# The split input of a feed-forward up-projection in lines of 128 bytes: high halves of 16 tokens beside their low halves

## The chip, the cores and the metric

One Trainium2 chip, one core. The time of a kernel is the device time of one execution in microseconds (us); the number that counts is the median over runs. A profiled execution gives a trace, and the page and the answers quoted here are read from it. Engines are named as the profile names them: PE (matrix engine, matmuls), PEld (its weight loads), DVE (vector), ACT (scalar), POOL (GpSimd), SP (the queue that issues most transfers).

## What is computed

One decoder layer on 256 tokens of 2048 features: two token mixers merged by gates, a cross-attention into 256 memory tokens, and a channel mixer. Each of the three adds a normed result to the residual stream. The change touches the channel mixer:

```python
def conv_glu_ffn(h, w_up, conv_w, conv_b, w_down):
    u = h @ w_up                                   # 256x2048 @ 2048x16384: the up-projection
    uc = conv_b + sum(conv_w[j] * shift_right(u, CONV_WIDTH - 1 - j) for j in range(CONV_WIDTH))
    gate, up = split_cols(uc, (D_FF, D_FF))        # D_FF = 8192
    return (jax.nn.gelu(gate, approximate=True) * up) @ w_down

h = rms_norm(x, ffn_pre_norm[l])
x = x + rms_norm(conv_glu_ffn(h, ...), ffn_post_norm[l])
```

Everything is float32.

## The kernel before

**Products in three parts.** Every large matrix product is split: an operand is stored as a high half, rounded to the type that the profile prints as fp32r (four bytes an element, as float32), and a low half, what the rounding left. A product is then three matmuls that add into one PSUM tile: high weights with high input, high weights with low input, low weights with high input. ACT makes the high half of the weights (`wh`, line 391), DVE the low half (`wl`, line 421).

**The stream of weights.** All weights pass PE once, in the order in which the program needs them, as pieces of 128 partitions by 1024 numbers (512 KB): `Feed` loads a piece (`raw`), and `hi` and `lo` split it into `wh` and `wl`. The pieces are counted from 0 through the whole program (`i` in `Feed.staged`). The order of work is written out by the program: `run()` goes through the blocks and issues matmuls, and `Spread` slips the other engines' work in between by a fixed budget. There is no scheduler behind it.

**The up-projection.** It is 32 blocks of kind "fm", each with eight pieces of 2 x 512 weights. Features lie on partitions: in each matmul 128 x 128 weights are the stationary operand, and 256 tokens of one group of 128 features are the moving operand. So there are 32 x 8 x 2 x 4 = 2048 weight tiles of each half, and 3 x 2048 = 6144 matmuls of 256 columns, each with a weight load of its own. The moving operands are the tiles `fh` and `fl` (high and low half of the normed residual stream): 16 groups of features x 256 tokens each, so that one matmul reads 256 numbers that follow each other, 1024 bytes in each partition. The same holds for the earlier "fm" blocks with `hh`, `hl` (mixers) and `mh`, `ml` (memory tokens).

**The down-projection** is of kind "tm": there the input (`as`) is stationary, and 512 columns of weights move.

**Where operands start.** The tiles of the moving inputs start at a multiple of 128 bytes. `Feed.staged` puts a piece of weights 16 numbers (64 bytes) into its buffer, so that weights of "fm" blocks start 64 bytes past a multiple of 128. For 19 pieces the table `KICK` moves them: by 24 numbers (96 bytes) instead of 16, or with eight numbers more between the two groups of features in the piece, or both.

```python
o = 0 if c >= 512 and self.kind[i] == "tm" else 16
if kick is not None:
    o, e = ((24, e + 24), (o, e + 8), (24, e))[kick]
```

None of the 19 pieces belongs to the up-projection (pieces 264 to 519).

**What makes fh and fl.** When the cross-attention's statistic is there, `Residual.run` scales and adds the residual stream group by group: ACT writes the high half (`act.activation`), DVE the low half (`scalar_tensor_tensor`). The very first group is made in two halves of the tokens by DVE alone, since PE waits for it. `Residual.tile(k)` hands group k to the matmuls. After the up-projection the buffers of `fh` and `fl` (tag `hT`, two buffers) are used again for the last norm's gain and for half of its result (`z3`).

Of the kernel before, what the change touches and what calls it, by code (L numbers as in the profile page):

```python
# [9 lines left out]
F32 = mybir.dt.float32  # L10
F32R = mybir.dt.float32r
AF = mybir.ActivationFunctionType
# [3 lines left out]
P = 128  # L16
D = 2048
S = 256
# [127 lines left out]
def _layer(ctx, tc, nc, d, dbg):  # L146
# [15 lines left out]
    def big(name, shape=None, dt=F32):  # L162
        return mp.tile(shape or [P, KD, S], dt, tag="big", bufs=2, name=name)

    def hT(name):
        return mp.tile([P, KD, S], F32R, tag="hT", bufs=2, name=name)

    def C(name, tag, shape=None, dt=F32):
        return mp.tile(shape or [P, S], dt, tag=tag, bufs=1, name=name)
# [8 lines left out]
        return pp.tile(shape or [P, 512], F32, tag="aux", bufs=4, name=name)  # L178

    def mm(out, lhsT, rhs, start=True, stop=True):  # L180
        pe.matmul(out, lhsT, rhs, start=start, stop=stop, skip_group_check=True)  # L181

    def keep_warm(n):
# [13 lines left out]
    def pcol(n, i=0, w=1):  # L197
        return par[:, PC[n] + i:PC[n] + i + w]
# [395 lines left out]
        return [d[name][blk, c] for c in range(d[name].shape[1])]  # L594


    hh, hl = hT("hh"), hT("hl")
    xs0 = lambda k: (hh[:, k], hl[:, k])
    st0 = Stat("st0")

# [897 lines left out]
    def part(v, k2):  # L1498
        return v[k2 // 4][:, (k2 % 4) * 2:(k2 % 4) * 2 + 2]

    class Residual:
# [8 lines left out]
        def run(self):  # L1510
            st, key, hi, lo, gname = self.a
            z, xr = M[key], M["xr"]
            for _ in range(10):
                if st.done:
                    break
                yield
            while not st.done:
                side._piece(side.bulk[0])
            rb = st.rb
            if not self.early:  # L1520
                keep_warm(5)

            def parts(i, js=(0, 1)):
                for j in js:
                    k = i * 2 + j
                    act.activation(hi[:, k], part(xr, i)[:, j], AF.Identity, scale=pcol(gname, k))
                for j in js:
                    k = i * 2 + j
                    dve.scalar_tensor_tensor(lo[:, k], part(xr, i)[:, j], pcol(gname, k), hi[:, k],
                                             op0=ALU.mult, op1=ALU.subtract)  # L1530
                self.ready = i + 1

            def scale(i):
                dve.tensor_mul(part(z, i), part(z, i), bc(rb, 2))

            def add(i):
                dve.tensor_add(part(xr, i), part(xr, i), part(z, i))

            if self.early:
                yield  # L1540
            a, x = part(z, 0), part(xr, 0)
            for j in range(2):
                if j == 0 and not self.early:
                    for t in TH:
                        dve.tensor_mul(a[:, 0, t], a[:, 0, t], rb[:, t])
                    for t in TH:
                        dve.scalar_tensor_tensor(hi[:, 0, t], a[:, 0, t], pcol(gname, 0), M["xg"][:, 0, t],
                                                 op0=ALU.mult, op1=ALU.add)
                else:
                    dve.tensor_mul(a[:, j], a[:, j], rb)  # L1550
                dve.tensor_add(x[:, j], x[:, j], a[:, j])
                if j == 0 and not self.early:
                    dve.scalar_tensor_tensor(lo[:, 0], x[:, 0], pcol(gname, 0), hi[:, 0], op0=ALU.mult,
                                             op1=ALU.subtract)
            if self.early:
                scale(1)
                parts(0)
            else:
                parts(0, (1,))
                scale(1)  # L1560
            yield
            for i in range(1, 8):
                if i == 1:
                    add(1)
                if i < 7:
                    scale(i + 1)
                    add(i + 1)
                parts(i)
                if i == 1 and not self.early:
                    side.more()  # L1570
                if self.early:
                    self.st2.add(part(xr, i - 1))
                    if i == 7:
                        self.st2.add(part(xr, 7))
                        self.stats = side.add(self.st2.early_column(), chain=1, free=True)
                elif i == 6:
                    self.stats = side.add(self.squares(), chain=1)
                yield
# [48 lines left out]
    stm = Stat("stm", "ysb0")  # L1627

    def mem_prep():
        M["mh"], M["ml"] = hT("mh"), hT("ml")  # L1630
        ts = []
        for c in range(10):
            if c % 2 == 0 and c < 8:
                ts.append(C("mem", f"bg{c // 2 % 2}", [P, 4, S]))
                sp.dma_start(ts[c // 2], d["mem"][:, c * 2:c * 2 + 4])
            if c >= 2:
                t = ts[c // 2 - 1][:, c % 2 * 2:c % 2 * 2 + 2]
                for j in range(2):
                    k = c * 2 - 4 + j
                    split_gain(M["mh"][:, k], M["ml"][:, k], t[:, j], pcol("mg", k))  # L1640
                stm.add(t)
            yield
        yield from stm.finish()
# [164 lines left out]
    def start_ffn():  # L1808
        M["cv"] = C("cv", "ysb0", [P, 4, P])
        act.dma_start(M["cv"], d["conv"])  # L1810
        side.need(xo3["task"])
        M["res"] = Residual(st3, "z2", stf, hT("fh"), hT("fl"), "fg", False)

    M["ac"] = []

# [106 lines left out]
                yield  # L1922

    def load_gain():
        M["gain"] = mp.tile([P, D], F32, tag="hT", bufs=2, name="gain")
        sp.dma_start(M["gain"], d["fpg"].partition_broadcast(P))

    E4 = [slice(0, S), slice(S, 2 * S)]
# [1 line left out]
    def fd_evac(n):  # L1930

        def gen(ps):
            if n:
                z = mp.tile([P, 2, 1024], F32, tag="hT", bufs=2, name="z3")
            else:
                z = U("z3", [P, 2, 1024])
            M["z3", n] = z

            if n == 0:
                M["ssq"], M["rco"] = small("ssq", [P, 2, 4], bufs=1), small("rco", [P, 2], bufs=1)  # L1940
            ssq, rco = M["ssq"], M["rco"]

            def squares(g):
                jk = T2("jk", [P, 512])
                act.activation(jk, ps[g], AF.Square, accum_out=ssq[:, g // 2, n * 2 + g % 2:n * 2 + g % 2 + 1])

            def gain(g):
                c = slice(g % 2 * 512, g % 2 * 512 + 512)
                dve.tensor_mul(z[:, g // 2, c], ps[g], M["gain"][:, n * 1024 + c.start:n * 1024 + c.stop])

            def before_last(t):
                ss = M["sso"] = small("sso", [P, 1], bufs=2)
                dve.tensor_reduce(ss, ssq[:, t, 0:3], axis=AX.X, op=ALU.add)
                dve.tensor_scalar(ss, ss, 1.0 / D, EPS, op0=ALU.mult, op1=ALU.add)

            def finish(t):
                r = rco[:, t:t + 1]
                act.activation(r, ssq[:, t, 3:4], AF.Ln, scale=1.0 / D, bias=M["sso"])
                act.activation(r, r, AF.Exp, scale=-0.5)

            def result(t, c):
                f = slice(c % 2 * 512, c % 2 * 512 + 512)
                x, z_ = M["xt"][c // 2][:, t, f], M["z3", c // 2][:, t, f]
                if t and c == 0:
                    diag = C("diag", "ysb0", [P, P])
                    act.activation(diag, ident, AF.Copy, scale=rco[:, t:t + 1])
                    for q, v in zip(M["sum"], E4):
                        mm(q, diag, z_[:, v], start=False)
                    for q, v in zip(M["sum"], E4):
                        act.copy(x[:, v], q)  # L1970
                else:
                    dve.scalar_tensor_tensor(x, z_, rco[:, t:t + 1], x, op0=ALU.mult, op1=ALU.add)
                (act if t and c == 0 else sp).dma_start(d["out"][t, :, c * 512:c * 512 + 512], x)

            if n == 0:
                for g in range(4):
                    squares(g)
                    gain(g)
                    yield
                return  # L1980
            squares(0)
            before_last(0)
            gain(0)
            squares(1)
            finish(0)
            gain(1)
            result(0, 0)
            result(0, 1)
            squares(2)
# [12 lines left out]
            yield  # L2002
        return gen
# [97 lines left out]
```

## Time and profile before

| what | value |
|---|---|
| runs, median (lowest to highest) | 1866.33 us (1866.29 to 1867.76), 3 runs |
| profiled execution, first to last instruction | 1863.2 us |
| PE busy | 1853.5 us, 99% of the span |
| DVE, ACT, POOL busy | 1295.5, 1017.0, 32.4 us |
| granted PE clock, mean | 0.999 of full |
| up-projection, first to last matmul start | 806.6 to 1507.2 us |
| bytes read | 347.01 MB, 187 GB/s over the span |

The profiled execution has no time of its own in the list of runs; its span is 3.1 us below their median, and this rest, what lies before the first and behind the last instruction, is added to spans below to compare them with runs. Busy time of PE is no measure of its speed, since one matmul's recorded 276 ns overlaps the next two: what a matmul costs is the distance from one start to the next.

### The profile page before, as it was taken

The numbers are of one execution on the slowest core, as the hardware profiler recorded it, in microseconds if no ns is written. First come the engines' busy times: TensorE is split into PE (matmuls) and PEld (weight loads), VectorE is DVE, ScalarE is ACT, GpSimd is POOL, SyncE is SP. The second block draws the span as 40 slices with busy tenths as digits, with TensorE's granted clock in tenths as the row PEclk, the third lists the DMA queues.
The fourth block names the chain that finished last, engine by engine and source line by source line (L and its number), as shares of the span: only waits on it lengthen the run. The fifth ranks groups of instructions, "written<-read, shape, count | busy, mean of one in ns | idle before, by whom it ended". The sixth has DMA issues, their size and how long they took to land.

```text
span 1863.2 us, 36212 instructions
## 1 busy us (share of the span) xinstructions
PE 1853.5 (99%) x14934; PEld 1767.5 (95%) x14934; DVE 1295.5 (70%) x1832; ACT 1017.0 (55%) x1492; POOL 32.4 (2%) x62
## 2 busy tenths in 40 slices
PE   9999999999999999999999999999999999999998
PEld 9999988999999999999999999999999988888887
DVE  7789777566675857787766667776666775556555
ACT  6876445655454646665554455444445554545544
POOL 0000020000000000000000000000000000000000
PEclk9999999999999999999999999999999999999999
DMA  7556544344555765555666666666666666666664
GB/s 261 186 166 203 180 149 160 136 160 158 172 195 196 277 197 180 165 180 172 202 192 194 196 195 196 185 194 199 195 194 195 197 192 215 194 193 192 194 192 145
DMA packets 98198, 351.47 MB, mean 189 GB/s; under 512 B 11056, under 2 KB 11568, under 8 KB 97648
## 3 DMA queue, kind: packets, MB, share of 16 engines
q1 hardware_dynamic: 97168, 348.01, 58.6%
q8 instruction: 117, 1.92, 0.4%
q10 hardware_dynamic: 864, 1.15, 0.2%
q14 instruction: 49, 0.40, 0.1%
HBM read 347.01 MB, written 2.10 MB: 187 GB/s over the span
## 4 chain that ended last, share of the span: by engine, by line
PE 98%; DVE 1%; DMA 0%; issue 0%; ACT 0%; ACTq 0%; DVEq 0%
PE fm L181 68%; PE tm L181 25%; PE gram L181 0%; DVE wl L421 0%; PE Y L181 0%; DMA w<-in_w_in_dram 0%; PE num L181 0%; PE lv L181 0%; DVE ql L66 0%; PE X L181 0%; PE U L181 0%; PE zg L181 0%; DVE z L66 0%; PE zwa L181 0%; PE xsc L181 0%
## 5 line engine op out<-in xcount | busy, mean ns | idle before, releaser
L421 DVE TENSOR_TENSOR wl<-raw,wh 128x1024 fp32r<-128x1024 f32 (+1 forms) x639 | 774.8, 1218 | 412.7 <-ACT wh L391 406.5
L391 ACT CAST wh<-raw 128x1024 fp32r<-128x1024 f32 (+1 forms) x639 | 663.6, 1043 | 476.0 <-PE fm L181 362.5
L181 PE MATMUL fm<-fh,wh 128*128 128x256 f32 x2048 | 564.2, 277 | 0.6 <-DVE fh L66 0.6
L181 PE MATMUL fm<-fh,wl 128*128 128x256 f32 x2048 | 563.2, 276 | 0.0
L181 PE MATMUL fm<-fl,wh 128*128 128x256 f32 x2048 | 563.2, 276 | 0.0
L181 PEld LDWEIGHTS fm<-fh,wh 128*128 128x128 f32 x2048 | 383.6, 188 | 0.8 <-DVE fh L66 0.8
L181 PEld LDWEIGHTS fm<-fl,wh 128*128 128x128 f32 x2048 | 383.5, 188 | 0.0
L181 PEld LDWEIGHTS fm<-fh,wl 128*128 128x128 f32 x2048 | 383.5, 188 | 0.0
L181 PE MATMUL tm<-wh,as 128*128 128x512 f32 x1024 | 315.1, 389 | 0.0
L181 PE MATMUL fm<-hh,wh 128*128 128x256 f32 x1024 | 284.3, 280 | 1.7 <-ACT wh L402 1.5
L181 PE MATMUL fm<-hl,wh 128*128 128x256 f32 x1024 | 281.7, 277 | 0.0
L181 PE MATMUL fm<-hh,wl 128*128 128x256 f32 x1024 | 281.5, 277 | 0.1
L181 PEld LDWEIGHTS tm<-wh,as 128*128 128x128 f32 x1024 | 192.2, 188 | 39.8
L181 PE MATMUL tm<-wl,as 128*128 128x512 f32 x512 | 199.2, 389 | 0.0
L181 PEld LDWEIGHTS fm<-hh,wh 128*128 128x128 f32 x1024 | 191.9, 188 | 3.4 <-ACT wh L402 1.7
L181 PEld LDWEIGHTS fm<-hl,wh 128*128 128x128 f32 x1024 | 191.9, 188 | 0.1
L181 PEld LDWEIGHTS fm<-hh,wl 128*128 128x128 f32 x1024 | 191.5, 188 | 0.3 <-DVE wl L421 0.3
L181 PEld LDWEIGHTS tm<-wl,as 128*128 128x128 f32 x512 | 96.1, 188 | 19.9
L66 ACT CAST as<-ac 128x256 fp32r<-128x256 f32 x128 | 45.6, 404 | 110.8 <-PE tm L181 110.8
L66 DVE TENSOR_TENSOR as<-ac,as 128x256 fp32r<-128x256 f32 x128 | 48.6, 421 | 61.7 <-ACT as L66 61.7
L181 PE MATMUL fm<-mgh,wh 128*128 128x256 f32 x256 | 70.9, 277 | 0.0
L181 PE MATMUL fm<-mgl,wh 128*128 128x256 f32 x256 | 70.8, 276 | 0.0
(406 smaller groups left out, 2225.0 us busy)
## 6 DMA issues: line engine op xcount, KB each, us to landing
raw<-in_w_fu_dram SPq DMA_DIRECT2D x256, 512.0 KB, 4.1
raw<-in_w_in_dram SPq DMA_DIRECT2D x152, 512.0 KB, 3.6
raw<-in_w_fd_dram SPq DMA_DIRECT2D x128, 512.0 KB, 3.9
raw<-in_w_br_dram SPq DMA_DIRECT2D x32, 512.0 KB, 4.1
raw<-in_w_mo_dram SPq DMA_DIRECT2D x32, 512.0 KB, 4.3
raw<-in_w_xk_dram SPq DMA_DIRECT2D x8, 512.0 KB, 4.2
raw<-in_w_xv_dram SPq DMA_DIRECT2D x8, 512.0 KB, 3.6
raw<-in_w_xq_dram SPq DMA_DIRECT2D x8, 512.0 KB, 4.0
```

The costliest lines, as they stand in the source:

```text
L66: return f(out, *a, **k)
L181: pe.matmul(out, lhsT, rhs, start=start, stop=stop, skip_group_check=True)
L391: nc.scalar.copy(wh, r)
L421: nc.vector.tensor_sub(wl, r, self.st[self.nl][0])
```

## The change

The two tiles of a split input become one tile of twice the size. For the mixers and for the memory tokens (`hpair`) the high half fills its first 16 KB of a partition and the low half its second, so a matmul reads there what it read before (1024 bytes in a row). For the up-projection (`hlines`) the tile is cut into lines of 32 numbers (128 bytes): 16 tokens' high halves in a line's first 64 bytes, the same tokens' low halves in its second. A matmul of the up-projection then reads 16 runs of 64 bytes, 128 bytes apart, in place of one run of 1024 bytes; `mm` gives its PSUM output the same shape of 16 x 16. What ACT and DVE write there has this pattern too, 16 runs of 16 numbers (8 runs in the first group's halves). The last norm's gain and `z3` become parts of one tile `hend` in the same place.

```diff
-    def hT(name):
-        return mp.tile([P, KD, S], F32R, tag="hT", bufs=2, name=name)
+    def hT(name, dt=F32R):
+        return mp.tile([P, 2 * KD * S], dt, tag="hT", bufs=1, name=name)
+
+    def hpair(name):
+        v = hT(name).rearrange("p (i k s) -> p i k s", i=2, k=KD)
+        return v[:, 0], v[:, 1]
+
+    def hlines(name):
+        v = hT(name).rearrange("p (k l i w) -> p i k l w", k=KD, i=2, w=W16)
+        return v[:, 0], v[:, 1]
+
+    W16 = 16
+
+    def lines(v):
+        return v.rearrange("p (l w) -> p l w", w=W16)
...
     def mm(out, lhsT, rhs, start=True, stop=True):
+        if len(rhs.shape) == 3 and len(out.shape) == 2 and rhs.shape[2] == W16:
+            out = lines(out)
         pe.matmul(out, lhsT, rhs, start=start, stop=stop, skip_group_check=True)
...
-    hh, hl = hT("hh"), hT("hl")
+    hh, hl = hpair("hp")
...
+            as_hi = (lambda v: v) if self.early else lines
...
-                    act.activation(hi[:, k], part(xr, i)[:, j], AF.Identity, scale=pcol(gname, k))
+                    act.activation(hi[:, k], as_hi(part(xr, i)[:, j]), AF.Identity, scale=pcol(gname, k))
...
-                    dve.scalar_tensor_tensor(lo[:, k], part(xr, i)[:, j], pcol(gname, k), hi[:, k],
+                    dve.scalar_tensor_tensor(lo[:, k], as_hi(part(xr, i)[:, j]), pcol(gname, k), hi[:, k],
                                              op0=ALU.mult, op1=ALU.subtract)
...
-                        dve.scalar_tensor_tensor(hi[:, 0, t], a[:, 0, t], pcol(gname, 0), M["xg"][:, 0, t],
+                        l = slice(t.start // W16, t.stop // W16)
+                        dve.scalar_tensor_tensor(hi[:, 0, l], lines(a[:, 0, t]), pcol(gname, 0), lines(M["xg"][:, 0, t]),
...
-        M["mh"], M["ml"] = hT("mh"), hT("ml")
+        M["mh"], M["ml"] = hpair("mp")
...
-        M["res"] = Residual(st3, "z2", stf, hT("fh"), hT("fl"), "fg", False)
+        M["res"] = Residual(st3, "z2", stf, *hlines("fp"), "fg", False)
...
-        M["gain"] = mp.tile([P, D], F32, tag="hT", bufs=2, name="gain")
+        M["hend"] = hT("hend", F32)
+        M["gain"] = M["hend"][:, 0:D]
...
-                z = mp.tile([P, 2, 1024], F32, tag="hT", bufs=2, name="z3")
+                z = M["hend"][:, KD * S:KD * S + 2048].rearrange("p (t c) -> p t c", t=2)
```

No instruction is added, removed or moved: on each of the five engines the same instructions stand in the same order and wait for the same engines. Only the shapes of operands differ, in 6144 matmuls, 15 ACT and 18 DVE instructions. `mh` and `ml` change places in memory. The weights and their places stay as they are.

More of the change, by code (lines that the diff above doesn't have):

```diff
@@ L1552, in run @@
                 if j == 0 and not self.early:
-                    dve.scalar_tensor_tensor(lo[:, 0], x[:, 0], pcol(gname, 0), hi[:, 0], op0=ALU.mult,
+                    dve.scalar_tensor_tensor(lo[:, 0], lines(x[:, 0]), pcol(gname, 0), hi[:, 0], op0=ALU.mult,
                                              op1=ALU.subtract)
```

## The prediction

> **What bounds the kernel now.** First the page, its busy line and its chain:
>
> ```profile
> span 1863.2 us, 36212 instructions
> ...
> PE 1853.5 (99%) x14934; PEld 1767.5 (95%) x14934; DVE 1295.5 (70%) x1832; ACT 1017.0 (55%) x1492; POOL 32.4 (2%) x62
> ...
> PE 98%; DVE 1%; DMA 0%; issue 0%; ACT 0%; ACTq 0%; DVEq 0%
> PE fm L181 68%; PE tm L181 25%; PE gram L181 0%; DVE wl L421 0%; PE Y L181 0%; DMA w<-in_w_in_dram 0%; PE num L181 0%; PE lv L181 0%; DVE ql L66 0%; PE X L181 0%; PE U L181 0%; PE zg L181 0%; DVE z L66 0%; PE zwa L181 0%; PE xsc L181 0%
> ```
>
> The end of the kernel is set by PE for 98% of the span. So the question is what one matmul of the up-projection costs. The answer for the tiles fh and fl counts them:
>
> ```profile
> L181 PE MATMUL fm<-fh,wh x2048: 276/276/467, 806.6 to 1506.9; 128*128 128x256 f32 x187
> L181 PE MATMUL fm<-fh,wl x2048: 276/276/283, 807.6 to 1507.2; 128*128 128x256 f32 x187
> L181 PE MATMUL fm<-fl,wh x2048: 276/276/282, 808.5 to 1507.0; 128*128 128x256 f32 x187
> L66 DVE SCALAR_TENSOR_TENSOR fl<-xr,par,fh x16: 477/479/486, 806.9 to 837.2; 128x256 fp32r<-128x256 f32 x16
> L66 ACT ACTIVATE fh<-xr,par x15: 493/497/511, 808.2 to 835.9; 128x256 fp32r<-128x256 f32 x15
> L66 DVE SCALAR_TENSOR_TENSOR fh<-z,par,xg x2: 345/346/346, 805.9 to 806.2; 128x128 fp32r<-128x128 f32 x2
> ```
>
> 6144 matmuls start between 806.6 and 1507.2 us: 700.6 us, or 114.0 ns each with all stalls. The undisturbed distance is read from two starts of the same kind in the timeline of PE:
>
> ```profile
> 1000.00 0.28 PE L181 MATMUL fm<-fh,wh 128*128 128x256 f32 x1
> ...
> 1006.80 0.28 PE L181 MATMUL fm<-fh,wh 128*128 128x256 f32 x1
> ```
>
> 60 matmuls (20 rounds of three) lie between them: 6.80 us / 60 = 113.3 ns. 6144 x 113.3 = 696.3 us, so only 4.3 us of the stage are stalls. The down-projection, with 512 columns, has nine rounds of three in this stretch:
>
> ```profile
> 1600.46 0.61 PE L181 MATMUL tm<-wh,as 128*128 128x512 f32 x2
> ...
> 1606.58 0.61 PE L181 MATMUL tm<-wh,as 128*128 128x512 f32 x2
> ```
>
> 6.12 us / 27 = 226.7 ns, twice 113.3. So a matmul costs 0.4427 ns for each column that moves and nothing beside. The windows show the granted clock and the weights' makers beside it:
>
> ```profile
> core 0: us, PE busy (x) PEld busy (x) DVE busy (x) ACT busy (x) POOL busy (x), PEclk, DMA share, GB/s
> 810.00:820.00 10.00, 10.00 (x91) 10.00 (x90) 9.90 (x15) 7.37 (x11) 0.00 (x0) 1.00 0.36 107
> 820.00:830.00 10.00, 10.00 (x91) 10.00 (x90) 9.93 (x15) 5.82 (x8) 0.00 (x0) 1.00 0.81 263
> 1000.00:1200.00 200.00, 200.00 (x1767) 200.00 (x1766) 137.36 (x182) 99.11 (x127) 0.00 (x0) 1.00 0.64 195
> ```
>
> The clock is full, and between 1000 and 1200 us DVE is idle for a third of the time and ACT for half of it. Nothing but PE's own pace sets this stage, and the change touches just that: how the moving operand lies while it is read.
>
> **What the trace says on places.** The same instructions do run at other paces here. Early in the up-projection there is a stretch with the same tiles at the same places:
>
> ```profile
> 855.43 0.28 PE L181 MATMUL fm<-fh,wh 128*128 128x256 f32 x1
> ...
> 858.61 0.28 PE L181 MATMUL fm<-fh,wh 128*128 128x256 f32 x1
> ...
> 858.97 0.60 PE L1920 MATMUL xt<-con,xr 128*128 128x128 f32 x4
> ...
> 859.76 0.28 PE L181 MATMUL fm<-fh,wh 128*128 128x256 f32 x1
> ...
> 860.10 0.28 PE L181 MATMUL fm<-fh,wh 128*128 128x256 f32 x1
> ```
>
> 3.18 us / 27 = 117.8 ns, until four transposes come in between; behind them a round takes 0.34 us again. So there are two ways of being in step, 4.4 ns apart. And two pieces that `KICK` moves by 32 bytes (numbers 18 and 216, both with kick 2; only the weights lie elsewhere):
>
> ```profile
> 50.93 0.28 PE L181 MATMUL fm<-hh,wh 128*128 128x256 f32 x1
> ...
> 53.45 0.28 PE L181 MATMUL fm<-hh,wh 128*128 128x256 f32 x1
> ```
>
> ```profile
> 661.33 0.28 PE L181 MATMUL fm<-mgh,wh 128*128 128x256 f32 x1
> ...
> 663.44 0.28 PE L181 MATMUL fm<-mgh,wh 128*128 128x256 f32 x1
> ```
>
> Seven rounds in 2.52 us are 120.0 ns a matmul, six in 2.11 us are 117.2 ns. The reading that I take from these rows: the weights of the next matmul are read while this one's input streams, the two streams hinder each other when they are in the same part of the memory's rows at once, and the 64-byte distance between them in the kernel before is what keeps them apart. The Trainium skill, TensorE: Matmul & The Clock Gate, section "Step-by-step: what each phase is for", says otherwise: two independent read ports, so that loading the next weights takes nothing from the running matmul. By that rule the place of the weights could not matter and the change would cost nothing; the 113.3, 117.2 and 120.0 ns disagree with it.
>
> **The change, part by part.**
>
> 1. *6144 matmuls read 16 runs of 64 bytes, 128 apart.* No row here has a moving operand in runs, so the price is bounded. A high half is now always in the first 64 bytes of a 128-byte line, a low half always in the second, while the weights still go through both halves in turn. Being apart all the time is then not possible: of every two 64-byte pieces of weights one lies in the half that is being read. Upper end: 120.0 - 113.3 = 6.7 ns a matmul, the worst of the rows, 6144 x 6.7 = 41 us. Lower end: a gain. The weight loads bound it:
>
> ```profile
> L181 PEld LDWEIGHTS fm<-fh,wl 128*128 128x128 f32 x2048 | 383.5, 188 | 0.0
> L181 PEld LDWEIGHTS U<-au,mt 64*64 64x64 f32 x128 | 4.0, 134 | 0.6 <-issue 0.3
> ```
>
> 64 columns more take 54 ns more, so 128 columns of weights take about 108 ns, and each matmul has its own load: below 108 the pace can't fall, a gain of at most 5.3 ns, 33 us. Between these ends I take half of the worst row, since half of the weights' pieces can meet the input: 3.35 ns, 6144 x 3.35 = 20.6 us. It lies near the three slower rows (3.9, 4.4 and 6.7 ns above 113.3) and on their lower side, because the steady 113.3 shows that the two streams, left alone, find a step in which they don't meet.
>
> 2. *18 DVE and 15 ACT instructions write in runs.* On the path are the two `fh` halves and the first `fl`, for which PE waits at 806 us: 2 x 0.346 + 0.479 = 1.2 us. If runs doubled them, 1.2 us more; as contiguous, 0; a gain would need a write in runs to be quicker than one in a row, so I set 0. I take 0.2. The other 16 DVE and 15 ACT instructions are beside the matmuls. Their cover is thin, DVE is busy for 9.90 and 9.93 of 10 us there, yet PE starts 91 matmuls in 10 us and keeps its pace, because pieces of weights are split ahead. Doubled they would add 15 x 0.48 = 7.2 us to DVE; with the cover gone that many us would end up in PE's wait for `wl`. I take 0 and keep 7 us as the end.
>
> 3. *One tile for two, `hend`, mh and ml in each other's place.* No wait is added: each engine waits for the same engines as before, and the matmuls of mixers and memory read the same 1024 bytes in a row. 0; what hides the gain's load is the half of the down-projection that runs before it is used, as before.
>
> 4. *Queues.* Nothing is moved past anything; SP's and POOL's rows are the same. 0.
>
> Sum: 1863.2 + 20.6 + 0.2 = 1884.0 us of span, and with the 3.1 us between span and median 1887.1 us, 1.1% over 1866.3.
>
> **The rivals.**
>
> *The layout does not matter (no change).* PE may fetch 64 bytes, or less, at a time; then 16 runs are the same 16 fetches. For it speaks the third block of matmuls whose moving operand (here the weights) starts 64 bytes into a line:
>
> ```profile
> 771.31 0.28 PE L181 MATMUL tm<-wh,mh 128*128 128x256 f32 x1
> ...
> 773.69 0.28 PE L181 MATMUL tm<-wh,mh 128*128 128x256 f32 x1
> ```
>
> 2.38 us / 21 = 113.3 ns, though it touches nine lines of 128 bytes and not eight. Against it are the 117 to 120 ns rows, which show that places count. It gives 1866.3, within 0.2% (3.7 us, about what a measurement of this kernel can tell from no change), which is 0.6 ns a matmul. The Trainium skill, SBUF — State Buffer, section "Door 1", puts the lines at 16 bytes, with a penalty for each crossing into a new one; 64-byte runs use all of a line, so by that rule the change is free too. The row above agrees with it; the two kicked pieces, at the same alignment to 16 bytes, do not.
>
> *The matmuls get faster (the other side).* The steady 113.3 ns may itself hold a loss, one that comes each time the moving read goes from one half of a line to the other, or each time it meets the weights. An input that stays in one half for a whole matmul would lose the first kind. Then the weight loads' 108 ns is the next bound: 1866.3 - 33 = 1833 us. It counts from 112.7 ns down (0.6 ns or more saved). For it: 113.3 and 226.7 are exactly in proportion to the columns at full granted clock, as a loss for every so many bytes would be. Against it: the down-projection pays the same 0.4427 ns a column while weights load in less than half of its time, so the loss would have to be of the first kind, and no row shows a moving operand that stays in one half. By the formula for a warm back-to-back gap in the Trainium skill, TensorE: Matmul & The Clock Gate, section "Back-to-back issue gap" (columns / 2.4 + 2.5 ns), 256 columns would take 109.2 ns, and the gain would be an estimated 25 us; no row here reaches that figure.
>
> *A fetch is a line of 128 bytes.* Then twice as many lines are fetched for the same numbers, and all weights' pieces can meet the input, not half of them. The nearest price is the whole of the worst row, 120.0 ns: 1866.3 + 41 = 1907 us. The row at 771 us speaks against it: one line more in eight cost nothing there.
>
> **How the numbers follow.** My forecast, streams that meet half of the time (2 to 4.5 ns a matmul, 1879 to 1895): 0.40. Lines of 128 bytes (1907): 0.10. No change: 0.27. Faster: 0.23. So slower 0.50, same 0.27, faster 0.23. The time is that of the likeliest, 1887. Its own range is 1879 to 1895; leaving out faster alone would leave out 0.23, so the range goes from the faster bound, 1832, to the upper end of part 1 with the little of part 2, 1908.
>
> **What would show it.** In the timeline of the changed kernel at 1000 us: 20 rounds in 7.0 us (116.7 ns) for the forecast, 6.80 for no change, 7.2 for whole lines, 6.5 for faster. High and low inputs should slow alike, the down-projection should keep 226.7 ns, and the writes of `fp` stay near 0.48 and 0.50 us. I am wrong if a stretch of thousands of matmuls still reads 113.3: then the two streams avoid each other in time and not by place. I am also wrong if the slower pace is there but changes at every interruption, as at 859 us: then it is the step, not the layout, that was hit.

## The result, and the profile after

The kernel before took 1866.31 us (median of 4 runs, 1864.25 to 1867.76), the changed one 1907.82 us (4 runs, 1907.45 to 1908.32). The ratio is 1.0224, with a 95% interval of 1.0209 to 1.0238: slower by 41.5 us, where 20.8 us were forecast. The page of the changed kernel shows the span, the busy time of the engines and the chain that ended last, by engine:

```profile
span 1906.5 us, 36212 instructions
...
PE 1896.8 (99%) x14934; PEld 1810.8 (95%) x14934; DVE 1297.3 (68%) x1832; ACT 1020.1 (54%) x1492; POOL 32.5 (2%) x62
...
PE 99%; DMA 0%; DVE 0%; ACT 0%; ACTq 0%; issue 0%; DVEq 0%
```

The same number of instructions, and PE is still the end of nearly everything. The span grew by 43.3 us, PE's busy time by as much, and DVE's and ACT's by 2 and 3 us. (The medians lie 41.5 us apart and the spans 43.3, because the profiled execution of before was shorter than its median run: in all runs on record that list both, the time is 1.7 to 1.9 us longer than the span. So of the 3.1 us that were set beside the span of before, some 1.3 are a difference between executions and not a rest that belongs to each.) The instructions on the tile `fp` (shortest, median and longest in ns, then first and last start) say where:

```profile
L196 PE MATMUL fm<-fp,wh x4096: 281/284/470, 806.5 to 1550.4; 128*128 128x256 f32 x196
L196 PE MATMUL fm<-fp,wl x2048: 281/283/286, 807.6 to 1550.6; 128*128 128x256 f32 x187
L66 DVE SCALAR_TENSOR_TENSOR fp<-xr,par,fp x16: 476/478/486, 806.8 to 838.7; 128x256 fp32r<-128x256 f32 x16
L66 ACT ACTIVATE fp<-xr,par x15: 492/497/509, 808.2 to 837.6; 128x256 fp32r<-128x256 f32 x15
L66 DVE SCALAR_TENSOR_TENSOR fp<-z,par,xg x2: 343/344/344, 805.9 to 806.1; 128x128 fp32r<-128x128 f32 x2
```

The up-projection starts at 806.5 us as before (806.6) and lasts to 1550.6 instead of 1507.2: its 744.1 us are 43.5 us more than the 700.6 before, which is the whole growth of the span. The writes in runs of 64 bytes take what writes in a row took (0.478 and 0.497 us, before 0.479 and 0.497). Windows at three places (the columns are those shown for before; the bracketed number behind PE counts its starts):

```profile
810.00:820.00 10.00, 10.00 (x85) 10.00 (x84) 9.90 (x15) 7.46 (x11) 0.00 (x0) 1.00 0.36 104
1000.00:1200.00 200.00, 200.00 (x1663) 200.00 (x1662) 130.28 (x173) 94.49 (x120) 0.00 (x0) 1.00 0.61 183
1600.00:1800.00 200.00, 200.00 (x884) 165.61 (x883) 120.61 (x152) 104.17 (x157) 0.00 (x0) 1.00 0.64 198
```

At a full granted clock PE started 1663 matmuls in 200 us of the up-projection, before 1767: 120.3 ns each against 113.2. In the down-projection both have 884. Over the second half of the stage the starts in the trace are 120.4 ns apart on the mean, before 113.3. 6144 x 7.1 ns = 43.6 us: the slower pace is the whole loss, and stalls stayed at some 4 us. The timeline, two rows 20 rounds of three matmuls apart (each row holds two matmuls, since high and low input are now one tile):

```profile
1000.01 0.40 PE L196 MATMUL fm<-fp,wh 128*128 128x256 f32 x2
...
1007.24 0.40 PE L196 MATMUL fm<-fp,wh 128*128 128x256 f32 x2
```

7.23 us / 60 = 120.5 ns. This is the row for which the prediction named 7.2 us for "whole lines", 7.0 for its own forecast and 6.8 for no change.

### The profile page after: what moved, and what is told of

Read it like the earlier page. It is cut to its first block, busy times and chain, and to the rows that moved or that the text cites. A ratio compares the mean times of both kernels' runs of the same rounds, so it can differ in the third digit from the quotient of the medians.

```text
span 1906.5 us, 36212 instructions
## 1 busy us (share of the span) xinstructions
PE 1896.8 (99%) x14934; PEld 1810.8 (95%) x14934; DVE 1297.3 (68%) x1832; ACT 1020.1 (54%) x1492; POOL 32.5 (2%) x62
## 4 chain that ended last, share of the span: by engine, by line
PE 99%; DMA 0%; DVE 0%; ACT 0%; ACTq 0%; issue 0%; DVEq 0%
PE fm L196 70%; PE tm L196 25%; PE gram L196 0%; PE Y L196 0%; DMA w<-in_w_in_dram 0%; PE num L196 0%; PE lv L196 0%; PE X L196 0%; PE U L196 0%; PE zg L196 0%; PE zwa L196 0%; PE xsc L196 0%; PE xt L1938 0%; PE stb L196 0%; PE Tn L196 0%; PE xo L196 0%
## 5 line engine op out<-in xcount | busy, mean ns | idle before, releaser
L196 PE MATMUL fm<-fp,wh 128*128 128x256 f32 x4096 | 740.1, 284 | 0.6 <-DVE fp L66 0.6
L196 PEld LDWEIGHTS fm<-fp,wh 128*128 128x128 f32 x4096 | 631.1, 188 | 0.9 <-DVE fp L66 0.8
L196 PE MATMUL fm<-fp,wl 128*128 128x256 f32 x2048 | 578.5, 284 | 0.0
L196 PEld LDWEIGHTS fm<-fp,wl 128*128 128x128 f32 x2048 | 385.0, 188 | 0.0
L196 PE MATMUL fm<-hp,wh 128*128 128x256 f32 x2048 | 353.8, 278 | 1.8 <-ACT wh L417 1.5
L196 PEld LDWEIGHTS fm<-hp,wh 128*128 128x128 f32 x2048 | 308.6, 188 | 3.5 <-ACT wh L417 1.7
L196 PE MATMUL fm<-hp,wl 128*128 128x256 f32 x1024 | 281.8, 277 | 0.1
L196 PEld LDWEIGHTS fm<-hp,wl 128*128 128x128 f32 x1024 | 191.6, 188 | 0.3 <-DVE wl L436 0.3
L196 PE MATMUL tm<-wh,hp 128*128 128x512 f32 (+1 forms) x320 | 93.0, 375 | 0.3 <-DVE qk L66 0.3
L196 PE MATMUL fm<-mgh,wl 128*128 128x256 f32 x256 | 70.8, 276 | 0.0
```

## The experiments

Eighteen kernels were run, in five sets, each set beside runs of the kernel before on the same chip, with medians of 1863.13 to 1864.94 us. `w32` and `b_o0` were run four times, the others once, so for these the argument rests on the pace in the trace and not on a few us of time. One row of each carries its verdict: the window from 1000 to 1200 us, in the midst of the up-projection, with PE's starts in it. 200 us divided by the starts is the pace; 1767 starts are the pace before, 1663 that of the change. The granted clock is full (1.00) in all of these rows. In the code cuts, `...` stands for lines left out.

For the places, the words used below: an address in a partition, modulo 256 bytes, falls into one of four quarters of 64 bytes (0, 64, 128, 192). In the built kernel before, `fh` and `fl` start at 128 and the weights of the up-projection at 192 (the operands' addresses in the built program; no trace shows them), and a matmul's 1024 bytes go through the quarters in order, four times. In the changed kernel a high half goes 128, 0, 128, 0 and so on, and a low half 192, 64, 192, 64.

### First set: length of a run, length of a load, number of columns

**`w32`**: runs of 32 numbers (128 bytes, in lines of 256).

```diff
-    W16 = 16
+    W16 = 32
```

> The changed kernel with runs of 32 numbers: lines of 256 bytes, high halves of 32 tokens in the first 128 bytes, low halves in the second. Theory of meetings (the prediction's: input that stays in one 64-byte half meets half of the weights' pieces): each run goes through both halves again, so the steady distance is 113.3 ns and the time 1866 to 1868 us. Theory of lines (a read pays for each line of 128 bytes that it opens, 16 instead of 8): eight whole lines again, 113.3 ns, 1866 to 1868 us. Theory of jumps (each break in the address costs, 7.1 ns for 15 breaks in a matmul): 7 breaks, 3.3 ns, 116.6 ns, 1887 us.

```profile
1000.00:1200.00 200.00, 200.00 (x1669) 200.00 (x1669) 129.69 (x173) 94.00 (x118) 0.00 (x0) 1.00 0.59 183
```

1904.50 us against 1864.04, ratio 1.0219 (1.0200 to 1.0237); 119.8 ns by the window, 120.0 over the stage's second half. A run now fills 128 bytes, and the number of breaks is halved, yet the loss is that of the change. None of the three theories gave this time. So it isn't that half of a 128-byte line is fetched in vain, and it isn't a price for each break.

**`w8`**: runs of 8 numbers (32 bytes, in lines of 64).

```diff
-    W16 = 16
+    W16 = 8
```

> The changed kernel with runs of 8 numbers: lines of 64 bytes, high halves of 8 tokens in the first 32 bytes, low halves in the second. Theory of lines of 128 bytes: a matmul opens 16 lines as in the changed kernel, 120.4 ns, 1908 us. Theory of jumps: 31 breaks, 113.3 + 14.7 = 128 ns, 1955 us. Theory of meetings: the read goes through both halves but at twice the pace of bytes, so it meets the weights at some of the pieces: 115 to 120 ns, 1877 to 1908 us.

```profile
1000.00:1200.00 200.00, 200.00 (x1701) 200.00 (x1700) 131.80 (x176) 97.43 (x124) 0.00 (x0) 1.00 0.61 188
```

1891.67 us, 117.6 ns. Twice as many breaks cost less, not more. A matmul here touches every quarter in order, half of each. Its low halves start 32 bytes later than its high ones, though, and that alone may be the loss: over the stage's second half the next matmul starts 116.7 ns behind one of a high half and 119.9 behind one of a low half, and in `c_lo64b` below, where nothing but a start differs, it is 116.7 and 120.0.

**`a_m32`**: the changed kernel, but two of the three matmuls of a round load 32 columns of weights, not 128 (the products of the other 96 are left out).

```diff
-  steps.append([(o, a, xh, first and m % 2 == 0, False), (o, c, xh, False, last),
-                (o, a, xl, False, False)])
+  n_ = 32 if b in fus and not first and not last and b not in entry else P
+  steps.append([(o, a, xh, first and m % 2 == 0, False), (o[0:n_], c[:, 0:n_], xh, False, last),
+                (o[0:n_], a[:, 0:n_], xl, False, False)])
...
```

> The changed kernel, but in 30 of the 32 blocks of the up-projection (without each block's first and last group of features) the two matmuls with a low half load only 32 columns of weights; the products of the other 96 columns with a low half are left out. The input is read just as in the changed kernel. Theories of lines and of jumps: the distance stays 120.4 ns whatever the loads are, 1908 us. Theory of meetings: a load of 32 columns meets a quarter as often, so two of three distances fall to 113.3 + 1.8 = 115 ns, the third stays at 120; 5040 of 6144 matmuls, 1908 - 18 = 1890 us.

```profile
1000.00:1200.00 200.00, 200.00 (x1669) 187.52 (x1667) 129.63 (x171) 93.24 (x118) 0.00 (x0) 1.00 0.59 184
```

1903.88 us, 119.8 ns. PE's loads are busy less (187.52 of 200 us), and nearly all of the loss stays. If the input lost time by meeting the weights' pieces, loads of a quarter of the length would have met it less.

**`tml`**: the kernel before, but the weights that move in the down-projection lie in lines of 128 bytes, high in a line's first half and low in its second.

```diff
+            if i >= 520:
+                v = t[:, 0:2 * k * c].rearrange("p (k l i w) -> p i k l w", k=k, i=2, w=16)
+                return v[:, 1 if lo else 0]
...
```

> The kernel before, with the weights of the down-projection (there they are the moving operand, 512 columns) in lines of 128 bytes, high halves of 16 columns in a line's first half, low halves in its second; the stationary input lies as before. All weight pieces share four double tiles. Theories of lines and of jumps: twice the runs of a matmul of 256 columns, 226.7 + 14.2 = 240.9 ns, 1536 x 14.2 = 22 us, 1888 us. Theory of meetings: a load is as long as with 256 columns, so it meets as often, 226.7 + 7.1 = 233.8 ns, 11 us, 1877 us.

Two views: the window in the up-projection, and the matmuls of the down-projection (their two rows in the kernel before, then the one row in this kernel).

```profile
L181 PE MATMUL tm<-wh,as x1024: 389/389/397, 1507.3 to 1855.0; 128*128 128x512 f32 x171
...
L181 PE MATMUL tm<-wl,as x512: 389/389/389, 1507.7 to 1855.2; 128*128 128x512 f32 x171
```

```profile
1000.00:1200.00 200.00, 200.00 (x1767) 200.00 (x1766) 137.00 (x182) 99.46 (x128) 0.00 (x0) 1.00 0.63 195
...
L188 PE MATMUL tm<-wpair,as x1536: 397/402/414, 1506.8 to 1878.6; 128*128 128x512 f32 x192
```

1888.31 us. The up-projection keeps its 1767 starts; the down-projection takes 371.8 us from first to last start instead of 347.9: 23.9 us on 1536 matmuls, some 15.5 ns each. That is a little over twice the 7.1 ns of 256 columns, though a matmul has one load of weights in both. In this run the loss goes with the columns that move, not with the loads.

### Second set: longer runs, and other arrangements

**`w64`** and **`w128`**: runs of 256 bytes in lines of 512, and of 512 in lines of 1024.

```diff
-    W16 = 16
+    W16 = 64      # w128: 128
```

> The changed kernel with runs of 64 numbers (256 bytes, 512 bytes from one to the next). Three theories are left after runs of 8, 16 and 32 numbers gave 117.8, 120.4 and 120.0 ns whatever the loads were. Breaks: a moving read that is not one piece costs about 6.7 ns, however many breaks: 120.0 ns, 1905 us. Blocks: what costs is how many blocks of memory a read opens, and a block is 256 bytes: then four whole blocks, as without lines, 113.3 ns, 1865 us; blocks of 512 bytes or more: 120.0. Places: high and low input start at different places (not a multiple of the same distance from each other), so successive matmuls are out of step: 120 or 117, 1890 to 1905 us.

> The changed kernel with runs of 128 numbers (512 bytes, 1024 from one to the next), one break in a matmul. Breaks: 120.0 ns, 1905 us. Blocks: 113.3 if a block is 512 bytes or less. Places: 117 to 120 ns.

The window's row of `w64`, and of `w128`:

```profile
1000.00:1200.00 200.00, 200.00 (x1767) 200.00 (x1767) 136.30 (x182) 100.19 (x128) 0.00 (x0) 1.00 0.63 194
```

```profile
1000.00:1200.00 200.00, 200.00 (x1767) 200.00 (x1766) 137.03 (x182) 99.81 (x128) 0.00 (x0) 1.00 0.63 195
```

1863.94 and 1865.83 us against 1864.94: the pace of before. A run of 256 bytes goes through all four quarters, one of 128 only through two. So interleaving as such costs nothing; in `w32` and the change, which lose, a matmul leaves quarters out.

**`kpair`**: lines of 128 bytes that hold two feature groups of the same half; so high and low input of a round start at the same quarter.

```diff
-        v = hT(name).rearrange("p (k l i w) -> p i k l w", k=KD, i=2, w=W16)
+        v = hT(name).rearrange("p (h k l i w) -> p h k i l w", h=2, k=KD // 2, i=2, w=W16)
...
+                return v[p, self.h, k // 2, k % 2][(slice(None),) + tuple(at[2:])]
...
```

> The changed kernel with lines of 128 bytes that hold two groups of features of the same half: 16 tokens of an even group in the first 64 bytes, of the next group in the second; high and low halves in regions of their own, 16 KB apart, so that the high and the low input of a weight tile start at the same place of a line. Runs, breaks and blocks are those of the changed kernel. Breaks and blocks: 120.4 ns, 1905 us. Places: 113.3 ns within a group, at most some extra at the change of group, 1864 to 1872 us.

```profile
1000.00:1200.00 200.00, 200.00 (x1650) 200.00 (x1649) 130.32 (x173) 93.75 (x121) 0.00 (x0) 1.00 0.59 182
```

1912.99 us, 121.2 ns. If it were their different starts that count, 113.3 ns were expected. That high and low start at different quarters is not what makes the lines slow.

**`c_lo64`**: no lines at all, each matmul reads 1024 bytes in a row, but the low half's region starts 64 bytes later (at 192).

```diff
+        hi = t[:, 0:n].rearrange("p (k l w) -> p k l w", k=KD, w=W16)
+        return hi, t[:, n + 16:2 * n + 16].rearrange("p (k l w) -> p k l w", k=KD, w=W16)
...
```

> The changed kernel without lines: high and low input of the up-projection each contiguous, 1024 bytes a matmul as before, but the low half's region starts 64 bytes past a multiple of 128 and not on it. Breaks and blocks: 113.3 ns, 1865 us. Places: the low input out of step with the high one, 117 to 120 ns, 1890 to 1905 us.

1908.86 us. It was not clean: its longer tile moved the tiles behind it by 128 bytes, among them the stationary input `as` of the down-projection, from 128 to 0. Its rows for the window and the down-projection:

```profile
1000.00:1200.00 200.00, 200.00 (x1700) 200.00 (x1700) 133.36 (x179) 97.78 (x125) 0.00 (x0) 1.00 0.62 187
...
L198 PE MATMUL tm<-wh,as x1024: 387/393/405, 1542.5 to 1899.0; 128*128 128x512 f32 x171
```

356.5 us from first to last start, where the kernel before has 347.7: the stationary operand's place, the only one of PE's operands there that moved, costs some 5.7 ns a matmul. The clean repeat is `c_lo64b`, below.

### Third set: which quarters, and in which order

All have runs of 64 bytes in the up-projection's input, at another pitch; the last is `c_lo64` with a tile that leaves the others in place.

**`p256`**: 256 bytes apart, so that a matmul stays in one quarter. **`p320`**: 320 apart, so that it goes through the quarters in order, though it jumps 15 times. **`p192`**: 192 apart, through the quarters in reverse.

```diff
-        v = hT(name).rearrange("p (k l i w) -> p i k l w", k=KD, i=2, w=W16)
+        v = hT(name).rearrange("p (g l s w) -> p g s l w", g=8, s=4, w=W16)                # p256
+        v = t[:, 0:30 * S].rearrange("p (g l s w) -> p g s l w", g=6, s=5, w=W16)          # p320
+        v = t[:, 0:30 * S].rearrange("p (g l s w) -> p g s l w", g=10, s=3, w=W16)         # p192
...
```

> The changed kernel with runs of 64 bytes 256 bytes apart: a line holds 16 tokens of four groups of features of the same half, high and low halves 16 KB apart, so the high and the low input of a weight tile start at the same place modulo 256. Theory of places modulo 256 (the memory of a partition works in four 64-byte places in turn, and a read is at full pace as long as it goes through them in order and in step with the weights): each matmul stays in one place, the worst there is, more than 121 ns, 1912 us or more. Theory of short runs (whatever comes in runs of less than 256 bytes costs 6.7 to 8 ns): 120 to 121.4 ns, 1905 to 1913 us.

> The same with runs of 64 bytes 320 bytes apart, five groups of features in a line, high and low input at the same place (the last group of features lies contiguous). Theory of places modulo 256: successive runs are at 0, 64, 128, 192, 0, ... modulo 256, the order of a read in one piece, so 113.3 ns in spite of 15 breaks, 1864 to 1868 us. Theory of short runs: 120 to 121.4 ns, 1905 to 1913 us.

> The same with runs of 64 bytes 192 bytes apart, three groups in a line (the last group contiguous): the places come in reverse order, 0, 192, 128, 64. Theory of places: all four places are used, but against the order of the weights, so the two meet: 116 to 121 ns, 1880 to 1910 us; 113.3 if the weights play no part. Theory of short runs: 120 to 121.4 ns.

The window's row of `p256`, of `p320` and of `p192`:

```profile
1000.00:1200.00 200.00, 200.00 (x1646) 200.00 (x1645) 130.02 (x172) 93.37 (x119) 0.00 (x0) 1.00 0.59 181
```

```profile
1000.00:1200.00 200.00, 200.00 (x1719) 200.00 (x1718) 134.50 (x180) 98.40 (x126) 0.00 (x0) 1.00 0.61 188
```

```profile
1000.00:1200.00 200.00, 200.00 (x1685) 200.00 (x1684) 130.30 (x171) 95.17 (x120) 0.00 (x0) 1.00 0.60 187
```

1913.88, 1882.83 and 1897.16 us; 121.5, 116.3 and 118.7 ns. The mean of `p320` hides two paces. A feature group is twelve matmuls; the timeline shows the first of three groups that follow each other (starting at quarter 128, then 192, then 0):

```profile
995.06 0.39 PE L208 MATMUL fm<-fp,wh 128*128 128x256 f32 x2
...
996.42 0.39 PE L208 MATMUL fm<-fp,wh 128*128 128x256 f32 x2
...
997.84 0.40 PE L208 MATMUL fm<-fp,wh 128*128 128x256 f32 x2
```

The group that starts at 128 takes 1.36 us / 12 = 113.3 ns, the pace of before with 15 jumps in each matmul; the next, which starts at 192, 1.42 / 12 = 118.3. So it goes on: groups that start at 192, 0 and 64 take 118.1 to 118.7 ns, one that starts at 128 takes 113.3, and 115.4 if it follows a slow one. The theory of places had expected 113.3 ns in all groups. Two things are needed at once here: the quarters in order, and a quarter to start with that fits. One quarter alone (`p256`) is hardly worse than two (`w32`, the change), so the loss isn't the number of reads that fall on one quarter.

**`c_lo64b`**: `c_lo64` with its tile 256 bytes longer than that of the change, in place of 128 (the cut is against `c_lo64`).

```diff
-        return mp.tile([P, 2 * KD * S + 32], dt, tag="hT", bufs=1, name=name)
+        return mp.tile([P, 2 * KD * S + 64], dt, tag="hT", bufs=1, name=name)
```

> The contiguous input with the low half's region 64 bytes past a multiple of 256 away from the high half's, now with the tile's size a multiple of 256 bytes longer, so that nothing else changes its place modulo 256 (in the run before, everything behind the tile lay 128 bytes further, and the down-projection went from 226.7 to 232 ns as well). Places: the up-projection still at 117 to 120 ns, all other stages as in the kernel before: 1888 to 1900 us. Short runs: 113.3 ns, 1865 us.

```profile
1000.00:1200.00 200.00, 200.00 (x1701) 200.00 (x1700) 132.12 (x175) 96.92 (x123) 0.00 (x0) 1.00 0.61 188
...
1600.00:1800.00 200.00, 200.00 (x884) 165.62 (x883) 120.53 (x152) 104.28 (x157) 0.00 (x0) 1.00 0.64 199
```

1892.22 us, 117.6 ns in the up-projection; the down-projection has its 884 starts back. An input that lies in a row, but in one third of the matmuls starts 64 bytes later, lengthens the stage from 700.6 to 728.5 us: 27.9 us, two thirds of what the change costs.

### Fourth set: the weights' place, and loads that are short everywhere

**`b_o0`** and **`b_o32`**: the kernel before, input in a row; only the weights of the up-projection start 64 bytes earlier (at 128, the input's quarter) or 64 bytes later (at 0).

```diff
             o = 0 if c >= 512 and self.kind[i] == "tm" else 16
+            if 264 <= i < 520:
+                o = 0         # b_o32: 32
```

> The kernel before with the weights of the up-projection (256 pieces) 64 bytes earlier: they start at the same place modulo 256 as the input, not 64 bytes further. The input is contiguous and where it was. If places count relative to the weights: about 118.4 ns as the second group with runs 320 bytes apart (same distance), 6144 x 5.1 = 31 us, 1895 us. If only the input's own order counts: 113.3 ns, 1864 to 1866 us.

> The same with the weights 64 bytes later than in the kernel before (128 bytes past the input's place, modulo 256). Relative to the weights: 118 to 119 ns, 1893 to 1898 us. Input's own order: 113.3 ns.

The window's row of `b_o0`, and of `b_o32`:

```profile
1000.00:1200.00 200.00, 200.00 (x1669) 200.00 (x1669) 129.71 (x171) 93.31 (x118) 0.00 (x0) 1.00 0.59 184
```

```profile
1000.00:1200.00 200.00, 200.00 (x1688) 200.00 (x1687) 130.79 (x172) 95.58 (x121) 0.00 (x0) 1.00 0.60 186
```

1904.25 us, ratio 1.0217 (1.0200 to 1.0234), and 1896.16 us: 119.8 and 118.5 ns. Moving nothing but the weights by 64 bytes costs nearly as much as the change (40.5 us), and in `b_o0` every distance of the stage's second half is 120 ns (119 once), where the change has a mixture. So where the weights lie, with the input left alone, has a price by itself. `b_o0` lost more than the 1895 us expected from `p320`'s group of the same distance (118.4 ns).

**`a_m32all`** and **`bo0_m32all`**: the changed kernel, and `b_o0`, with all three matmuls of a round loading 32 columns (the products of the other 96 are left out).

```diff
-  steps.append([(o, a, xh, first and m % 2 == 0, False), (o, c, xh, False, last),
-                (o, a, xl, False, False)])
+  n_ = 32 if b in fus and not first and not last and b not in entry else P
+  steps.append([(o[0:n_], a[:, 0:n_], xh, first and m % 2 == 0, False), (o[0:n_], c[:, 0:n_], xh, False, last),
+                (o[0:n_], a[:, 0:n_], xl, False, False)])
...
```

> The changed kernel (lines of 128 bytes) with all three matmuls cut to 32 columns of weights, in 30 of 32 blocks and without each block's first and last group; the products of the other 96 columns are left out there. If the lines' loss comes from meeting the loads: a quarter of the loads' bytes is left, 113.3 + 1.8 = 115 ns or less there, 1908 - 27 = 1881 us. If the moving read is slow by itself: 120 ns, 1904 to 1908 us.

> The kernel before with the weights 64 bytes earlier (as in b_o0) and the same cut to 32 columns of weights. If the loss of moved weights is a meeting with the loads: near 113.3 + a quarter of b_o0's loss there, 1870 to 1876 us. If it is no meeting: b_o0's pace, 1895 us.

The window's row of `a_m32all`, and of `bo0_m32all`:

```profile
1000.00:1200.00 200.00, 200.00 (x1655) 182.26 (x1654) 129.82 (x172) 93.42 (x118) 0.00 (x0) 1.00 0.58 182
```

```profile
1000.00:1200.00 200.00, 200.00 (x1696) 185.42 (x1695) 131.78 (x174) 96.57 (x123) 0.00 (x0) 1.00 0.60 187
```

1909.99 and 1893.50 us; 120.8 and 117.9 ns. The lines cost the same with short loads. The weights' other place costs less with them, but two thirds of its loss stay. The kernel before with such loads was not run, so how much of the 117.9 is the place and how much the loads is open; the 113.3 and a quarter of `b_o0`'s loss that two streams meeting at every load would give (1870 to 1876 us) did not come.

### Fifth set: do the lines want another place for the weights?

**`a_o0`** and **`a_o32`**: the changed kernel with the weights of `b_o0` and of `b_o32` (the same two lines).

> The changed kernel (lines of 128 bytes) with the weights of the up-projection 64 bytes earlier, at the same place modulo 256 as the first runs of the high halves. If the lines' loss is one of distance to the weights, another place must mend it at least for one of the two inputs: 113.3 to 117 ns, 1864 to 1890 us. If lines lose by themselves because they skip two of four places: 120 to 122 ns, 1903 to 1915 us.

> The same with the weights 64 bytes later than in the changed kernel. Distance: 113.3 to 117 ns here or in a_o0. Lines by themselves: 120 to 122 ns, 1903 to 1915 us.

The window's row of `a_o0`, and of `a_o32`:

```profile
1000.00:1200.00 200.00, 200.00 (x1659) 200.00 (x1658) 129.76 (x172) 93.19 (x118) 0.00 (x0) 1.00 0.59 182
```

```profile
1000.00:1200.00 200.00, 200.00 (x1654) 200.00 (x1653) 130.06 (x173) 94.43 (x121) 0.00 (x0) 1.00 0.59 182
```

1908.48 and 1911.71 us, 120.6 and 120.9 ns, against 120.3 for the change. With the weights at 128, 192 or 0 the lines are equally slow: they lose by themselves, and not because one of these places fits them badly. The fourth place, 64, was not run.

## Why the prediction was right or wrong

**The step that failed** is number 1 of the sum, its price of 3.35 ns for a matmul. The direction, the stage and the resource were right: all of the loss is PE's pace in the up-projection. But the mean price is 7.1 ns, a little over the 6.7 that the step gave as its upper end, and the reading behind the half ("half of the weights' pieces can meet the input") is wrong. In that picture shorter loads meet the input less and cost less; with the lines they did not (`a_m32` 119.8 ns, `a_m32all` 120.8). Nor does a run of 128 bytes help, which goes through both 64-byte halves again as the weights do (`w32`: 113.3 ns by that picture, 120.0 measured). The row to take was the one that the sum gave as its bound: the piece at 50.93 us, 120.0 ns, where an operand lay at another place and nothing else. The reason to stay below it ("the two streams, left alone, find a step") is contradicted by `b_o0`, which stays at 120 ns for the whole second half of the stage. What the runs showed in the step's place: the lines lose by reading the 64-byte quarters out of order, whatever the loads do and wherever the weights were put, and they lose 7.1 ns. That 1907.8 us still lie inside the stated range (to 1908) is luck: the stage grew by 43.5 us where the range's upper end had 41, and the 3.1 us counted between span and median were 1.3 too many.

**The stretch at 855 us** was read as two ways of being in step, 4.4 ns apart. The runs bear out the values: 117.8 and 120.0 ns come again as means over half of the stage (`w8` and `c_lo64b` the first, `w32` and `b_o0` the second; in `b_o0` each distance is 120). What they add is that places can hold such a pace for thousands of matmuls. But they don't decide alone: that stretch, and the first blocks of `w128` (117.8 ns too, until other matmuls come between), run at the slower pace with the same places that give 113.3 ns later, and `bo0_m32all` has a short stretch of 113.3 ns at places that give 117.8.

**The rival "a fetch is a line of 128 bytes"** had the time (1907), by taking the whole of the worst row, but not the cause: `w32` uses its 128 bytes fully and loses as much, and a matmul of `p320` has its 16 runs in 16 different lines of 128 bytes and, where it starts at 128, loses nothing.

**The rival "no change"** fell, and with it the use of the row at 771 us. Its moving operand lies in a row, so that all quarters come in order; it says nothing on a reading that skips some. On the start it says more than was taken from it. In the built kernel that block's moving weights start at 192 and its stationary `mh` and `ml` at 128, and the block holds 113.3 ns at 771 us, but with the same places another pace eleven us earlier:

```profile
760.62 0.28 PE L181 MATMUL tm<-wh,mh 128*128 128x256 f32 x1
...
762.74 0.28 PE L181 MATMUL tm<-wh,mh 128*128 128x256 f32 x1
```

2.12 us / 18 = 117.8 ns. So a moving operand that starts one quarter after the stationary one, and not before it as in the up-projection, can hold 113.3 ns too, while `p320`'s groups at that distance (0 against 192) take 118.1. The Trainium skill, SBUF — State Buffer, section "Door 1", speaks of 16-byte lines; 64-byte runs fill them, and the 7.1 ns of the change disagree with that rule as a full account, as does `b_o0`, where nothing but a start place changes.

**The rival "faster"** fell: none of these kernels has a steady pace below 113.3 ns at 256 columns, and `p256`, whose matmuls stay in one quarter, is among the slowest (121.5).

**The Trainium skill's rule of two independent read ports** (TensorE: Matmul & The Clock Gate, section "Step-by-step: what each phase is for") was put aside in the prediction for the kicked pieces' sake. `b_o0` bears this out: the weights moved by 64 bytes, 40.5 us over the kernel before. That the two reads meet is not shown by it, since a quarter of the loads left two thirds of that loss (`bo0_m32all`, 117.9 ns). The change itself does not go against the rule: the lines are slow whatever the loads do (`a_m32all`, 120.8 ns).

**Parts 2 to 4** held. The writes in runs take the time of before, the first matmul starts at 806.5 us, the down-projection keeps its pace, and stalls in the stage stayed at 4 us. The sign that high and low inputs slow alike is there in part: the matmuls of the high half with high weights, low with high, and high with low weights follow each other by 119.2, 121.3 and 120.8 ns on the mean over the stage's second half.

**What is shown, and what stays open.** Shown, for 256 columns and weights that start at 192: PE settles at 113.3 ns where the moving operand goes through the four 64-byte quarters in order and starts at 128 (before, `w64`, `w128`, groups of `p320`). Breaking the order costs 5 to 8 ns (the change, `w32`, `p256`, `p192`, `kpair`), and so does another start in order, where it is held for a whole group of features (the other groups of `p320`, 4.8 to 5.4 ns) or for the weights (`b_o0`, `b_o32`, 6.7 and 5.4); `c_lo64b`, with one matmul in three at another start, loses 4.5 on the mean. Not shown: a rule for which start fits. The distance between the two operands is not enough for one, by the block at 771 us, and at 512 columns both operands at 128 take 226.7 ns while `c_lo64` with the stationary one at 0 takes 232.3. Open too: what in the memory or in PE makes it so, why the paces lie where they do, and what lets one pace turn into another at an interruption. No version ran faster than the kernel before by more than its runs differ; `w64` equals it.

## What to carry to other kernels

When PE is at its pace limit, look at where its operands lie modulo 256 bytes: here a moving operand in runs of 256 bytes, from the start that it had in a row, cost nothing, in shorter runs that skip quarters it cost 6% of the stage, and so did 64 bytes in the place of the weights. A trace that holds the same instruction at two paces gives the price of a bad place; here the whole of the worst row, and not a share of it, was near the price of a layout that nothing on record had tried. And before a mechanism is used to halve a price, ask which row shows the half.

## What the runs showed of the hardware that was not expected

- Breaks in the moving operand are free in themselves: 15 jumps in each matmul, from run to run 320 bytes, 113.3 ns (`p320`, groups that start at 128); 64-byte runs 128 apart, 120.4 ns (the change); 32-byte runs 64 apart, 117.8 ns (`w8`).
- The place of the stationary operand costs matmul time: 64 bytes earlier 6.7 ns of 113.3, 64 bytes later 5.4 ns (118.7 ns, the mean over the second half of the stage in `b_o32`).
- In runs of 64 bytes, 128 apart, a matmul loses 7.1 ns at 256 moving columns and some 15.5 ns at 512 (`tml`).
- Loads of 32 columns instead of 128 bring next to nothing with the lines: 119.8 and 120.8 ns against 120.3 (`a_m32`, `a_m32all`).
- The same instructions with the same places hold 113.3 ns in one stretch and 117.8 in another (771 and 761 us of the kernel before).
